# Folding the dt rows of an SSD layer to 128 partitions and moving two groups of transposes back in PE's queue

## The chip, the cores and the metric

The kernel runs on one core of one Trainium2 chip. The metric is device time in microseconds (us), the median over runs. All data are float32; the large products are done in three float32r matmuls (below).

## What is computed

A decoder trunk of two layers on 256 tokens with 2048 channels. Each layer is an RMSNorm with shift and scale from a conditioning vector (adaLN), a token mixer, an output projection, an adaLN gate and the residual sum. Layer 0 is a Mamba-2 SSD layer of 64 heads, layer 1 an xLSTM mLSTM layer of 8 heads. The part of the reference that the change touches is the step size dt of layer 0 and the decay that comes from it, in chunks of 128 tokens:

```python
proj = h @ w_in
z, xbc, dt = jnp.split(proj, [SSD_D_INNER, SSD_D_INNER + SSD_CONV_DIM], axis=-1)
dt = jax.nn.softplus(dt.astype(F32) + dt_bias.astype(F32))        # 256 tokens x 64 heads
a = -jnp.exp(a_log.astype(F32)).reshape(SSD_GROUPS, SSD_HEADS_PER_GROUP) * dt
y = ssd_chunked_scan(xs * dt[..., None], a, bmat, cmat)
# in the scan, for each chunk:
acs = jnp.cumsum(ac, axis=1)
decay = jnp.exp(jnp.where(causal, acs[:, :, None] - acs[:, None, :], -jnp.inf))
w_end = jnp.exp(total[:, None] - acs)
```

In layer 1 the input gate and the forget gate, one value per token and head, go through a log-sigmoid, a running sum and a running maximum in the same manner.

## The kernel before

**Tiling.** Weights stream from DRAM in tiles of 128x2048 floats, each loaded as two halves (`raw`, 128x1024). A half is split into two float32r parts: ACT copies it to `hi`, DVE subtracts to get `lo` (`split`, L270). A product is three matmuls: hi x h-hi, hi x h-lo, lo x h-hi (L304 to L306 with channels on the partitions, "fm"; L315 to L317 with tokens on the partitions, "tm"). There are six buffers for `raw` and four each for `hi` and `lo`. A half of an fm tile is 24 matmuls of 256 columns, a half of a tm tile 12 of 512.

**Units.** A `Unit` is one output block. It accumulates in two PSUM banks (the dt and gate units in one) of the pool `pj` or of the pool `ms` (function `misc()`), which have four banks each; small work shares `ms`: transposes, statistics, broadcasts. While the activations `h` of a layer come in four parts (adaLN scales arrive late), units are "parked": after each tile their two `ms` banks are added to a tile in SBUF by DVE (`park`, L86).

**Order.** The program is one list `items` of weight tiles, adaLN tiles and h parts. The main loop walks it half by half, issues loads and splits ahead, and before each half's matmuls steps every background generator once (`run_bg`). `yield` and `lag(n)` in a generator thus say how many halves later its next piece is issued. A scheduler then sets the order on each engine, and every engine takes its queue in order. The generators of the SSD heads wait by name (`held["dt"].over` and so on).

**The dt unit.** `dt_done` (L547) runs when the dt unit's 48 matmuls into one `pj` bank are issued. Its generator adds the bias and runs `softplus` (L413) on a 128x256 tile `dtrow`, of which only partitions 0 to 63 carry heads. One step later it multiplies by -exp(alog), scans each chunk of 128 tokens into `acs`, stores `acs` to DRAM (`acd`, POOL's queue) from where rows come back broadcast over partitions (`acb`, `gen_rows`), and computes `cr`, the distance to the chunk's end. One step after that come five PE transposes (L570 to L572) into two `ms` banks, and DVE copies them to `dtT` and `acT`, the per-token columns that `gen_decay` (ACT, tiles `E`) and `gen_ssd` (tiles `X`) use as scale and bias.

**The gate unit.** `gates_done` (L847) does the same for layer 1's gates: softplus on `gaterow`, scans, and after `lag(6)` four transposes (L872, L873) into two `ms` banks, read by ACT (`eT`) and DVE (`ncT`).

**Layer 1's moved products.** 16 adaLN tiles of layer 1 (`late`) are not loaded before layer 1 but dealt out between its first tiles, by the line with `n = ...` in the last loop over `items`.

## Time and profile before

| | us |
|---|---|
| median of 3 runs (1779.36 to 1780.19) | 1780.16 |
| the profiled execution | 1770.52 |
| its span, first to last instruction | 1768.7 |
| PE busy in it | 1679.2 |
| mean granted clock of PE | 0.98 of full |

The profile is of one execution. The span is what its rows add up to; 1.8 us of the profiled time lie around it. PE is the matmul engine, PEld its weight loads, DVE the vector engine, ACT the scalar engine, POOL and SP mostly issue DMAs here. [...] A row of the view in order of time gives start, duration, engine, line, operation, names out<-in, and in brackets how long the engine had been idle and who ended that. Durations of neighbours overlap by their pipeline's tail, so what an operation costs in a queue is the distance of two starts.

### The profile page before, as it was taken

The numbers are of one execution on the slowest core, as the hardware profiler recorded it, in microseconds if no ns is written. First come the engines' busy times: TensorE is split into PE (matmuls) and PEld (weight loads), VectorE is DVE, ScalarE is ACT, GpSimd is POOL, SyncE is SP. The second block draws the span as 40 slices with busy tenths as digits, with TensorE's granted clock in tenths as the row PEclk, the third lists the DMA queues.
The fourth block names the chain that finished last, engine by engine and source line by source line (L and its number), as shares of the span: only waits on it lengthen the run. The fifth ranks groups of instructions, "written<-read, shape, count | busy, mean of one in ns | idle before, by whom it ended". The sixth has DMA issues, their size and how long they took to land.

```text
span 1768.7 us, 32784 instructions
## 1 busy us (share of the span) xinstructions
PE 1679.2 (95%) x13285; PEld 1623.4 (92%) x13285; DVE 1301.9 (74%) x1639; ACT 923.3 (52%) x1551; POOL 35.6 (2%) x55
## 2 busy tenths in 40 slices
PE   2998979999999999989998999999999999999997
PEld 2998969998999999989888989899999898989997
DVE  7889978998986888867977986766556565564554
ACT  3443558788874674444445554544344444454433
POOL 0000000000000000000000000000000000000000
PEclk6999989999999999999999999999999999999998
DMA  9989745686876667958974567777555555565551
GB/s 358 338 311 320 275 161 179 213 280 226 280 284 207 220 219 254 337 167 307 328 249 153 203 229 246 254 246 246 182 181 178 181 175 184 188 196 169 189 180 71
DMA packets 111048, 405.20 MB, mean 229 GB/s; under 512 B 12440, under 2 KB 12448, under 8 KB 110896
## 3 DMA queue, kind: packets, MB, share of 16 engines
q1 hardware_dynamic: 107568, 391.50, 64.6%
q0 software_dynamic: 3040, 10.56, 2.0%
q8 instruction: 104, 1.70, 0.4%
q10 hardware_dynamic: 288, 1.05, 0.1%
q14 instruction: 48, 0.39, 0.1%
HBM read 400.89 MB, written 2.17 MB: 228 GB/s over the span
## 4 chain that ended last, share of the span: by engine, by line
PE 73%; issue 9%; DVE 8%; DMA 7%; ACT 2%; POOL 0%; SPq 0%; POOLq 0%; DVEq 0%; ACTq 0%
PE pj L304 18%; PE pj L305 18%; PE pj L306 18%; DMA raw<-in_ada 4%; DVE aacc L82 3%; DVE lo L86 3%; PE ms L304 2%; PE ms L305 2%; PE ms L306 2%; PE pj L315 2%; PE pj L317 2%; PE pj L316 2%; DMA raw<-in_wml 1%; ACT hi L78 1%; PE ms L697 1%
## 5 line engine op out<-in xcount | busy, mean ns | idle before, releaser
L78 ACT ACTIVATE hi<-raw 128x1024 fp32r<-128x1024 f32 x548 | 580.0, 1061 | 647.5 <-PE pj L305 394.0
L86 DVE TENSOR_TENSOR lo<-raw,hi 128x1024 fp32r<-128x1024 f32 x548 | 667.5, 1221 | 328.9 <-ACT hi L78 326.0
L304 PE MATMUL pj<-hT,hi 128*128 128x256 f32 x2144 | 605.3, 283 | 9.0 <-ACT hT L78 6.4
L305 PE MATMUL pj<-hT,hi 128*128 128x256 f32 x2144 | 600.3, 280 | 0.6 <-DVE hT L82 0.6
L306 PE MATMUL pj<-hT,lo 128*128 128x256 f32 x2144 | 600.0, 280 | 0.1
L304 PEld LDWEIGHTS pj<-hT,hi 128*128 128x128 f32 x2144 | 405.1, 189 | 12.2 <-ACT hT L78 7.2
L305 PEld LDWEIGHTS pj<-hT,hi 128*128 128x128 f32 x2144 | 405.1, 189 | 1.2 <-DVE hT L82 0.8
L306 PEld LDWEIGHTS pj<-hT,lo 128*128 128x128 f32 x2144 | 404.8, 189 | 0.3 <-DVE lo L86 0.3
L304 PE MATMUL pj<-y,hi 128*128 128x256 f32 x1024 | 291.4, 285 | 0.0
L306 PE MATMUL pj<-y,lo 128*128 128x256 f32 x1024 | 289.8, 283 | 0.0
L305 PE MATMUL pj<-y,hi 128*128 128x256 f32 x1024 | 289.8, 283 | 0.0
L82 DVE SCALAR_TENSOR_TENSOR aacc<-raw,cond,aacc 128x1024 f32<-128x1024 f32 x180 | 230.4, 1280 | 54.1 <-DMA raw<-in_ada 52.7
L304 PE MATMUL ms<-hT,hi 128*128 128x256 f32 x704 | 199.8, 284 | 9.4 <-ACT hi L78 3.3
L305 PE MATMUL ms<-hT,hi 128*128 128x256 f32 x704 | 197.6, 281 | 0.0
L306 PE MATMUL ms<-hT,lo 128*128 128x256 f32 x704 | 197.2, 281 | 0.0
L304 PEld LDWEIGHTS pj<-y,hi 128*128 128x128 f32 x1024 | 196.4, 192 | 0.5 <-issue 0.5
L305 PEld LDWEIGHTS pj<-y,hi 128*128 128x128 f32 x1024 | 196.5, 192 | 0.2 <-issue 0.2
L306 PEld LDWEIGHTS pj<-y,lo 128*128 128x128 f32 x1024 | 196.4, 192 | 0.0
L304 PEld LDWEIGHTS ms<-hT,hi 128*128 128x128 f32 x704 | 133.7, 190 | 12.1 <-ACT hi L78 4.6
L305 PEld LDWEIGHTS ms<-hT,hi 128*128 128x128 f32 x704 | 133.7, 190 | 0.3
L306 PEld LDWEIGHTS ms<-hT,lo 128*128 128x128 f32 x704 | 133.4, 190 | 0.0
L315 PE MATMUL pj<-hi,hT 128*128 128x512 f32 x192 | 76.5, 399 | 0.0
(186 smaller groups left out, 1549.3 us busy)
## 6 DMA issues: line engine op xcount, KB each, us to landing
raw<-in_wml SPq DMA_DIRECT2D x256, 512.0 KB, 4.2
raw<-in_ada SPq DMA_DIRECT2D x192, 512.0 KB, 5.3
raw<-in_wss SPq DMA_DIRECT2D x160, 512.0 KB, 4.8
raw<-in_wso SPq DMA_DIRECT2D x64, 512.0 KB, 5.8
raw<-in_wmo SPq DMA_DIRECT2D x64, 512.0 KB, 3.7
acb<-acd POOLq DMA_DIRECT2D x16, 512.0 KB, 5.6
xT<-in_xt SPq DMA_DIRECT2D x4, 512.0 KB, 5.9
raw<-in_wdt SPq DMA_DIRECT2D x2, 512.0 KB, 5.7
```

Of the source, the lines that this page charges most:

```text
L78: nc.scalar.activation(out, in_, func, **kw)
L82: nc.vector.scalar_tensor_tensor(out, a, s, b, op0, op1)
L86: nc.vector.tensor_tensor(out, a, b, op)
L304: nc.tensor.matmul(o, hi[:, w0:w0 + P], ah, start=first, stop=False, skip_group_check=True)
L305: nc.tensor.matmul(o, hi[:, w0:w0 + P], al, start=False, stop=False, skip_group_check=True)
L306: nc.tensor.matmul(o, lo[:, w0:w0 + P], ah, start=False, stop=last, skip_group_check=True)
L315: nc.tensor.matmul(o, ah[:, s], wh, start=(fresh and kk == 0), stop=False)
L316: nc.tensor.matmul(o, al[:, s], wh, start=False, stop=False)
L317: nc.tensor.matmul(o, ah[:, s], wl, start=False, stop=(kk == u.nk - 1 and (closes or (u.park is not None and ends))))
L697: nc.tensor.matmul(o, X[:, 0, xh, :], E[:, h, 0:T], start=True, stop=False, skip_group_check=True)
```

## The change

It does three things.

1. **dt.** After the bias, tokens 128 to 255 of the 64 heads are copied by ACT to partitions 64 to 127. `softplus`, the product with exp(alog) (now with the sign in the same operation, and exp(alog) copied to the upper partitions too) and the scan then run on 128x128. The scan's result lies in `dtrow` instead of `acs`; the store to DRAM is two stores of 64x128. The five transposes are three. They are issued after `lag(4)` instead of one step.
2. **Gates.** `lag(6)` becomes `lag(8)`.
3. **Layer 1's moved products.** The divisor of the line `n = ...` is smaller by 2.

```diff
--- before.py
+++ after.py
@@ -411,8 +411,9 @@
         return hT[:, k, 0:T], hT[:, k, T:2 * T]
 
     def softplus(x, out):
+        n = out.free_size()
         w = sp.tile([P, 3, T], F32, tag="e6", name=nm("spw"))
-        e, z, z2 = w[:, 0, :], w[:, 1, :], w[:, 2, :]
+        e, z, z2 = w[:, 0, 0:n], w[:, 1, 0:n], w[:, 2, 0:n]
         stt(e, x, -1.0, x, ALU.mult, ALU.min)
         act(e, e, AF.Exp)
         vts(z, e, 2.0, None, ALU.add)
@@ -537,7 +538,6 @@
 
     dtT = cp.tile([P, 2, 64], F32, tag="dtT", name="dtT")
     acT = cp.tile([P, 3, 64], F32, tag="acT", name="acT")
-    acs = cp.tile([P, T], F32, tag="rowA", name="acs")
     acd = dr.tile([64, T], F32, tag="acd", name="acd")
     dsk = cp.tile([P, 32], F32, tag="dskh", name="dskh")
     vts(dsk, vec("dsk", 0, 32), 0.5, None, ALU.mult)
@@ -548,32 +548,30 @@
         def g():
             bk = banks[0][:, 0:T]
             rw = sp.tile([P, 4, T], F32, tag="a4", name="dtrow")
-            dt, tmp = rw[:, 0, :], rw[:, 1, :]
-            vts(tmp, bk, vec("dtb"), None, ALU.add)
-            softplus(tmp, dt)
-            yield
-            na = sp.tile([P, 1], F32, tag="na", name="na", bufs=1)
-            act(na, vec("alog"), AF.Exp)
-            vts(na, na, -1.0, None, ALU.mult)
-            vts(tmp, dt, na, None, ALU.mult)
+            pre, dt, tmp, cr = rw[:, 0, :], rw[:, 1, 0:P], rw[:, 2, 0:P], rw[:, 3, 0:P]
+            acs = rw[:, 3, P:T]
+            vts(pre, bk, vec("dtb"), None, ALU.add)
+            act(pre[64:128, 0:P], pre[0:64, P:T], AF.Copy)
+            na = sp.tile([P, 2], F32, tag="na", name="na", bufs=1)
+            act(na[:, 0:1], vec("alog"), AF.Exp)
+            act(na[64:128, 0:1], na[0:64, 0:1], AF.Copy)
+            yield
+            softplus(pre[:, 0:P], dt)
+            stt(tmp, dt, -1.0, na[:, 0:1].broadcast_to([P, P]), ALU.mult, ALU.mult)
+            nc.vector.tensor_tensor_scan(acs, ones, tmp, 0.0, ALU.mult, ALU.add)
             for c in range(2):
-                s = slice(c * P, (c + 1) * P)
-                nc.vector.tensor_tensor_scan(acs[:, s], ones, tmp[:, s], 0.0, ALU.mult, ALU.add)
-            nc.gpsimd.dma_start(acd, acs[0:64, :])
+                nc.gpsimd.dma_start(acd[:, c * P:(c + 1) * P], acs[64 * c:64 * c + 64, :])
             slots.update(a4=1, e6=2)
             spawn(gen_rows())
-            cr = tmp[:, 0:P]
-            vts(cr, acs[:, 0:P], -1.0, acs[:, P - 1:P], ALU.mult, ALU.add)
-            yield
+            vts(cr, acs, -1.0, acs[:, P - 1:P], ALU.mult, ALU.add)
+            yield from lag(4)
             p1, p2 = misc(), misc()
-            for c in range(2):
-                nc.tensor.transpose(p1[:, c * P:(c + 1) * P], dt[:, c * P:(c + 1) * P], ident)
-                nc.tensor.transpose(p2[:, c * P:(c + 1) * P], acs[:, c * P:(c + 1) * P], ident)
-            nc.tensor.transpose(p2[:, 2 * P:3 * P], cr, ident)
+            nc.tensor.transpose(p1[:, 0:P], dt, ident)
+            nc.tensor.transpose(p2[:, 0:P], acs, ident)
+            nc.tensor.transpose(p2[:, P:T], cr, ident)
             give("a4")
-            vts(dtT, p1[:, 0:T].rearrange("p (c h) -> p c h", c=2)[:, :, 0:64],
-                                    0.5, None, ALU.mult)
-            nc.vector.tensor_copy(acT, p2[:, 0:384].rearrange("p (c h) -> p c h", c=3)[:, :, 0:64])
+            vts(dtT, p1[:, 0:P].rearrange("p (c h) -> p c h", c=2), 0.5, None, ALU.mult)
+            nc.vector.tensor_copy(acT, p2[:, 0:192].rearrange("p (c h) -> p c h", c=3))
             spawn(gen_decay())
             yield
         held["dt"] = spawn(g())
@@ -866,7 +864,7 @@
             nc.vector.tensor_tensor_scan(G, ip, ip, 0.0, ALU.max, ALU.max)
             nc.gpsimd.dma_start(Gd, G[0:8, :])
             vtt(lf, bc, G, ALU.add)
-            yield from lag(6)
+            yield from lag(8)
             p1, p2 = misc(), misc()
             for c in range(2):
                 nc.tensor.transpose(p1[:, c * P:(c + 1) * P], lf[:, c * P:(c + 1) * P], ident)
@@ -1012,7 +1010,7 @@
             if q == 3 and j == GPOS:
                 add_unit(Unit("fm", 1, 8, 1, h_act, gates_done), [wgt])
             items.append(w)
-            n = -(-len(late) // max(1, len(new) - j + (2 - q) * len(new))) if q < 3 and (q, j) >= (0, 3) else 0
+            n = -(-len(late) // max(1, len(new) - j + (2 - q) * len(new) - 2)) if q < 3 and (q, j) >= (0, 3) else 0
             items.extend(late[:n])
             late = late[n:]
     assert not late
```

What the built program makes of it is shown at three places, in the order of each engine's queue. Names carry buffer numbers, which differ between the two programs.

PE around the dt transposes, before (`pj340` is the dt unit's bank, `ms367` the first bank of the next tile, `hi350` its first half):

```order
L304 MATMUL pj340_2256<-hT_74,hi330_2188 128x256
L305 MATMUL pj340_2256<-hT_74,hi330_2188 128x256
L306 MATMUL pj340_2256<-hT_74,lo331_2189 128x256
L570 MATMUL ms355_2408<-ident_75,dtrow_2317 128x128 x2
L571 MATMUL ms356_2409<-ident_75,acs_164 128x128 x2
L572 MATMUL ms356_2409<-ident_75,dtrow_2317 128x128
L304 MATMUL ms367_2493<-hT_74,hi350_2363 128x256
L305 MATMUL ms367_2493<-hT_74,hi350_2363 128x256
```

And changed; between the dt unit and the first row here stand 44 matmuls of the next tile (`ms364`, `ms365`, halves `hi349` and `hi352`):

```order
L306 MATMUL ms365_2483<-hT_74,lo353_2400 128x256
L304 MATMUL ms365_2483<-hT_74,hi352_2399 128x256
L305 MATMUL ms365_2483<-hT_74,hi352_2399 128x256
L306 MATMUL ms365_2483<-hT_74,lo353_2400 128x256
L569 MATMUL ms370_2524<-ident_75,dtrow_2316 128x128
L570 MATMUL ms371_2525<-ident_75,dtrow_2316 128x128
L304 MATMUL ms376_2570<-hT_74,hi358_2438 128x256
L305 MATMUL ms376_2570<-hT_74,hi358_2438 128x256
L306 MATMUL ms376_2570<-hT_74,lo359_2439 128x256
L571 MATMUL ms371_2525<-ident_75,dtrow_2316 128x128
L304 MATMUL ms376_2570<-hT_74,hi358_2438 128x256
```

The transposes have moved behind two halves, 48 matmuls, and the third stands three matmuls behind the other two.

DVE in the softplus of dt, before (`spw` is softplus's work tile, `bc` and `xs` are convolutions of other units):

```order
L419 RECIPROCAL spw347_2319<-spw347_2319 128x256
L82 SCALAR_TENSOR_TENSOR bc365_2485<-th375_2565,bc365_2485 128x512
L86 TENSOR_TENSOR spw347_2319<-spw347_2319 128x256
L82 SCALAR_TENSOR_TENSOR xs354_2403<-pj60_300,V_72,xs354_2403 128x254
L86 TENSOR_TENSOR spw347_2319<-spw347_2319 128x256
L82 SCALAR_TENSOR_TENSOR xs354_2403<-pj60_300,V_72,xs354_2403 128x253
L90 TENSOR_SCALAR spw347_2319<-spw347_2319 128x256
L82 SCALAR_TENSOR_TENSOR bc365_2485<-pj68_362,V_72,bc365_2485 128x254
L82 SCALAR_TENSOR_TENSOR spw347_2319<-spw347_2319 128x256
L82 SCALAR_TENSOR_TENSOR bc365_2485<-pj68_362,V_72,bc365_2485 128x253
L82 SCALAR_TENSOR_TENSOR spw347_2319<-spw347_2319 128x256
L82 SCALAR_TENSOR_TENSOR xs354_2403<-th383_2617,xs354_2403 128x512
```

And changed, from the same operation on:

```order
L420 RECIPROCAL spw351_2354<-spw351_2354 128x128
L86 TENSOR_TENSOR lo369_2513<-raw347_2346,hi368_2512 128x1024
L86 TENSOR_TENSOR spw351_2354<-spw351_2354 128x128
L86 TENSOR_TENSOR park87_498<-park87_498,ms364_2482 128x512
L86 TENSOR_TENSOR spw351_2354<-spw351_2354 128x128
L86 TENSOR_TENSOR park87_498<-park87_498,ms365_2483 128x512
L90 TENSOR_SCALAR spw351_2354<-spw351_2354 128x128
L86 TENSOR_TENSOR lo374_2560<-raw348_2348,hi373_2559 128x1024
L82 SCALAR_TENSOR_TENSOR spw351_2354<-spw351_2354 128x128
L82 SCALAR_TENSOR_TENSOR bc362_2474<-th375_2563,bc362_2474 128x512
L82 SCALAR_TENSOR_TENSOR spw351_2354<-spw351_2354 128x128
L82 SCALAR_TENSOR_TENSOR xs354_2403<-pj60_299,V_72,xs354_2403 128x253
```

Every softplus operation is 128 wide, and two `lo` subtractions and two `park` additions stand between them, where convolution steps stood. Before, the corresponding subtractions and additions followed the transposes.

PE around the gate transposes, before (`ms1489`, `ms1490` belong to the tile before, `ms1501` to the next one):

```order
L316 MATMUL ms1490_11084<-hi1476_11004,hT_74 128x512
L317 MATMUL ms1490_11084<-lo1477_11005,hT_74 128x512
L872 MATMUL ms1498_11130<-ident_75,gaterow_10854 128x128
L873 MATMUL ms1499_11131<-ident_75,ip_10855 128x128
L872 MATMUL ms1498_11130<-ident_75,gaterow_10854 128x128
L873 MATMUL ms1499_11131<-ident_75,ip_10855 128x128
L304 MATMUL ms1501_11141<-hT_74,hi1483_11041 128x256
```

And changed, where 48 matmuls of the next tile (`ms1499`, `ms1500`) come first, and the tile after it (`ms1509`) follows:

```order
L305 MATMUL ms1500_11132<-hT_74,hi1486_11072 128x256
L306 MATMUL ms1500_11132<-hT_74,lo1487_11073 128x256
L870 MATMUL ms1507_11199<-ident_75,gaterow_10852 128x128
L871 MATMUL ms1508_11200<-ident_75,ip_10853 128x128
L870 MATMUL ms1507_11199<-ident_75,gaterow_10852 128x128
L871 MATMUL ms1508_11200<-ident_75,ip_10853 128x128
L315 MATMUL ms1509_11211<-hi1493_11099,hT_74 128x512
L316 MATMUL ms1509_11211<-hi1493_11099,hT_74 128x512
```

ACT at the same place, before:

```order
L78 ACTIVATE hi1493_11101<-raw1471_10971 128x1024
L78 ACTIVATE hi1496_11126<-raw1472_10973 128x1024
L78 ACTIVATE th1500_11138<-qk1488_11078 128x512
L78 ACTIVATE v1495_11123<-park1246_9433 128x512 x2
L78 ACTIVATE eT_169<-ms1498_11130 128x16
L78 ACTIVATE EP1529_11309<-Gb1507_11179,ncT_170 128x256
L78 ACTIVATE EP1529_11309<-Gb1507_11179,ncT_170 128x128
```

And changed:

```order
L78 ACTIVATE hi1493_11099<-raw1471_10969 128x1024
L78 ACTIVATE hi1496_11124<-raw1472_10971 128x1024
L78 ACTIVATE hi1503_11161<-raw1481_11035 128x1024
L78 ACTIVATE th1498_11128<-qk1488_11076 128x512
L78 ACTIVATE v1495_11121<-park1246_9431 128x512 x2
L78 ACTIVATE hi1505_11195<-raw1482_11037 128x1024
L78 ACTIVATE eT_168<-ms1507_11199 128x16
L78 ACTIVATE qk1517_11238<-park1267_9548,V_72 128x256 x3
```

`hi1503` stands ahead of the `v` copies and `hi1505` ahead of `eT`, and no `EP` operation, which waits for a DMA, stands right behind `eT`. Of the four `ms` banks, `ms1509` takes the one of `ms1507`, which `eT` reads.

On the load queue (SP) the two programs have the same order.

## Rows read from the trace of the kernel before

**Rows 1.** The page, part 1: busy us (share of the span) xinstructions.
```profile
PE 1679.2 (95%) x13285; PEld 1623.4 (92%) x13285; DVE 1301.9 (74%) x1639; ACT 923.3 (52%) x1551; POOL 35.6 (2%) x55
```

**Rows 2.** Waits, PE: engine line <- releaser: us in total, times, longest us.
```profile
PE ms L570 <- DVE dtrow L82: 12.9, 1, 12.9
...
PE ms L872 <- DVE gaterow L86: 5.3, 1, 5.3
```

**Rows 3.** Order of time, PE, 220 to 242: start us, us, instruction [idle before <-releaser].
```profile
220.86 0.36 PE L304 MATMUL pj<-hT,hi 128*128 128x256 f32 x1
...
226.43 0.27 PE L306 MATMUL pj<-hT,lo 128*128 128x256 f32 x1
239.59 0.69 PE L570 MATMUL ms<-ident,dtrow 128*128 128x128 f32 x2 [12.89 <-DVE dtrow L82]
...
241.09 0.56 PE L304 MATMUL ms<-hT,hi 128*128 128x256 f32 x1
```

**Rows 4.** Order of time, DVE, 226 to 242.
```profile
226.74 0.48 DVE L90 TENSOR_SCALAR dtrow<-pj,V 128x256 f32<-128x256 f32 x1 [0.20 <-PE pj L306]
227.14 0.47 DVE L82 SCALAR_TENSOR_TENSOR bc<-pj,V,bc 128x254 f32<-128x254 f32 x1
227.53 0.42 DVE L82 SCALAR_TENSOR_TENSOR spw<-dtrow 128x256 f32<-128x256 f32 x1
227.87 1.22 DVE L86 TENSOR_TENSOR lo<-raw,hi 128x1024 fp32r<-128x1024 f32 x1
229.00 0.29 DVE L90 TENSOR_SCALAR spw<-spw 128x256 f32<-128x256 f32 x1
229.20 0.47 DVE L82 SCALAR_TENSOR_TENSOR bc<-pj,V,bc 128x253 f32<-128x253 f32 x1
229.59 1.74 DVE L419 RECIPROCAL spw<-spw 128x256 f32<-128x256 f32 x1
231.25 0.63 DVE L82 SCALAR_TENSOR_TENSOR bc<-th,bc 128x512 f32<-128x512 f32 x1
...
239.12 0.42 DVE L82 SCALAR_TENSOR_TENSOR dtrow<-dtrow,spw 128x256 f32<-128x256 f32 x1
...
239.96 0.74 DVE L561 TENSOR_TENSOR_SCAN acs<-ones,dtrow 128x128 f32<-128x128 f32 x2
```

**Rows 5.** Order of time, PE, 956 to 971.
```profile
956.95 0.40 PE L317 MATMUL ms<-lo,hT 128*128 128x512 f32 x1
962.68 0.44 PE L872 MATMUL ms<-ident,gaterow 128*128 128x128 f32 x1 [5.33 <-DVE gaterow L86]
...
963.41 0.56 PE L304 MATMUL ms<-hT,hi 128*128 128x256 f32 x1
...
970.71 0.40 PE L315 MATMUL ms<-hi,hT 128*128 128x512 f32 x1
```

**Rows 6.** Order of time, DVE and ACT, 957 to 964.
```profile
962.46 0.67 DVE L86 TENSOR_TENSOR park<-park,ms 128x512 f32<-128x512 f32 x1
963.05 1.21 DVE L86 TENSOR_TENSOR lo<-raw,hi 128x1024 fp32r<-128x1024 f32 x1
...
957.20 1.06 ACT L78 ACTIVATE hi<-raw 128x1024 fp32r<-128x1024 f32 x1 [1.47 <-issue]
...
963.16 0.63 ACT L78 ACTIVATE v<-park 128x512 f32<-128x512 f32 x1 [0.30 <-DVE park L86]
963.70 0.17 ACT L78 ACTIVATE eT<-ms 128x16 f32<-128x16 f32 x1
```

**Rows 7.** Stretches: from:to us, length, busy us of five engines, PEclk, DMA share, GB/s.
```profile
245.00:480.00 235.00, 229.90 (x1966) 223.66 (x1964) 212.15 (x279) 195.34 (x441) 13.77 (x17) 1.00 0.70 236
417.00:424.00 7.00, 4.41 (x41) 3.89 (x40) 7.00 (x10) 3.70 (x9) 0.00 (x0) 1.00 0.87 270
962.60:966.90 4.30, 4.22 (x20) 4.25 (x21) 4.30 (x10) 0.96 (x3) 1.63 (x3) 0.50 0.41 122
```

**Rows 8.** Order of time, ACT, 247 to 252.
```profile
247.87 1.57 ACT L78 ACTIVATE E<-acb,acT 128x128 f32<-128x128 f32 x5 [1.73 <-DMA acb<-acd]
```

## The prediction

> **What bounds the kernel.** [...] The page's busy times come first: PE, the matmul engine, is busy for 95% of the span, DVE for 74% and ACT for 52% [rows 1]. A change pays here only where it removes time in which PE stands still, or in which it runs at its lower clock. Next, PE's waits, longest single wait first: two of them are for operands that this change touches, 12.9 us before the first dt transpose and 5.3 us before the first gate transpose [rows 2]. Both are single events. In PE's own order of time [rows 3, 5] one sees that PE had its next matmuls ready on both occasions: they follow the transposes without a further wait. So PE, which takes its queue in order, stood behind a transpose while work that did not need it was queued after it. [...]
>
> **The dt place, as it was.** The last dt matmul starts at 226.43, the first transpose at 239.59, the first matmul of the next tile at 241.09 [rows 3]. In between DVE is never idle: it works off the softplus, 256 columns an operation, with convolution steps of other blocks in between, from 226.74 to the last softplus step at 239.12 [rows 4].
>
> **The dt place, changed.** Two things happen. Half the columns: 128 partitions carry 128 tokens each. And by `lag(4)` 48 matmuls, two halves of a weight tile, now stand ahead of the first transpose. All four split halves lie ready (the matmuls after 241.09 ran on without a wait [rows 3]), so PE does these 48 in what was idle time. Their price: the dt unit is itself 48 such matmuls, from 220.86 to 226.43 plus one step, 5.6 us [rows 3].
>
> But the scheduler also drew other work forward into DVE's queue: two more `lo` subtractions and two `park` additions stand before the softplus ends. I price DVE's new queue, from the bias to the last softplus step, by start-to-start times of [rows 4]: the bias 0.40; eight convolution steps at 0.39, 3.1; three `lo` at 1.13, 3.4; two `park` additions at 0.59 [rows 6], 1.2; two silu products at 0.63, 1.3; two scalar steps at up to 0.20, 0.4; ten softplus steps of 128 columns; one reciprocal. No row shows 128 columns in those steps. 256 columns cost 0.34 [rows 4], which is the upper bound, and half of that, 0.17, the lower. The 512-column product and the 256-column step differ by 0.21 in duration [rows 4], so 128 columns less are worth about 0.12: I take 0.22, in all 2.2. The reciprocal costs 1.66 now, and I take half, 0.85. Sum 12.9; with 0.15 for the copy that folds the upper tokens (ACT's queue; between 0.17, a 128x16 operation [rows 6], and 0.31, a fifth of 1.57 [rows 8], mostly hidden behind two convolution steps) the last step begins at 239.8 where it began at 239.12. It is shorter by 0.12 until its result is there, so the first transpose comes 0.5 us later than before.
>
> The second transpose waits once more: DVE does the copy of dt and then the scan between the two, some 1.3 us with the first transpose's own time, plus 0.2 for the second. That makes 1.5 from the first transpose to matmul number 49. Before, it took 1.5 from 239.59 to 241.09 [rows 3] to matmul number 1. The third transpose, three matmuls later, costs 0.2 at the low clock. Gain at this place: 5.6 - 0.5 - 0.2 = **4.9 us**. If 128 columns cost as much as 256, the ten steps and the reciprocal are 2.0 longer: 2.9. If they cost half, 0.5 shorter: 5.4.
>
> [...]
>
> **The gate place.** The last matmul of the tile before starts at 956.95, the gate transposes at 962.68, and the next tile's 48 matmuls last from 963.41 to 970.71 [rows 5]: 7.3 us, because the clock was at 0.50 until 966.9 [rows 7]. With `lag(8)` these 48 come first. They begin at 957.3 at the full clock and end at 962.9. DVE had the transposes' operand ready for 962.68 [rows 5], and the addition that frees the second of their banks ends at about 963.1 [rows 6], so the transposes run almost at once, to 963.5. Then a new wait stands at the next tile: its first PSUM bank is that of a gate transpose, and is free when ACT has read `eT`. On ACT the second `v` copy still ends at 963.8 (its wait on DVE's second bank is unchanged), then one `hi` split now stands ahead of `eT`: about 1.0, and 0.17 for `eT` [rows 6]. PE goes on at 964.9 instead of 970.71. Gain **5.8 us**. It would be 7.2 without the new wait, and 3.7 if the next tile had to wait for both banks of the tile before, which DVE adds up only by about 967.
>
> **What costs nothing.** Layer 1's moved products: 16 late loads are dealt out over the tiles from the fourth on, as many per tile as a ceiling of (left)/(tiles left) gives. That is 16/21, 15/20 and so on before, 16/19, 15/18 and so on now; every one rounds up to 1. The order on the load queue is unchanged, so this edit does nothing. On POOL there is one more store of dt rows; what follows it is priced under the rivals. The two tiny additions at the start on ACT are bounded by 0.17 each [rows 6] and lie beside the wait for x. Behind both places PE is the bound (229.9 of 235 us with DMA at 0.70, [rows 7]), so what is gained stays gained; loads start when DVE or ACT frees their buffers, and move along.
>
> **Sum.** 4.9 + 5.8 = 10.7 us. The profiled execution took 1770.52, so it would take 1759.8; the median of the runs is 9.6 higher than the profiled one, which I carry over: 1780.16 - 10.7 = **1769.5**.
>
> **Rivals.**
> (a) The dt chain is as long per step as with 256 columns: gain 2.9 + 5.8, 1771.5. For it: nothing here shows 128 columns in these steps. Against it: 512 and 256 columns do differ. 12%.
> (b) The new short wait of 1.4 us at the gates, followed by another tile, brings the low clock back. In the rows of before it did not: the stretch with 2.6 us of no matmul kept 1.00 [rows 7]. If it did, the cost is that of the stretch after the old wait, half of 4.3 us: 2.1, so 1771.6. [...] 8%.
> (c) Layer 0's SSD work after dt is dealt out anew over all queues. PE now loses 5.1 us between 245 and 480 [rows 7]; a less lucky order could lose as much again: 1774.6. A luckier one could save half: 1767. 13% for the unlucky one.
> (d) The waits only change place, to the banks or to the second transpose, and under 3.6 us is left: about 1778. 7%.
> (e) Slower. ACT's queue holds, after dt, twelve E operations that wait for the dt rows to come back from DRAM, and the `hi` splits behind them. Those rows arrived at 247.87 [rows 8], 7.2 after the scan. Now the scan is later by about 0.7, and a second store goes first. PE has five halves, some 14 us, before it needs the split behind the E operations, which take about 4 us to get through: the rows may come by 251.5, some 2 us of slack. Each further microsecond costs one. To be slower by more than 0.2% (3.6 us, about what a measurement can tell from no change) they must be 16 us late; at 20 us the time is 1784. Nothing in the rows comes near it. 4%.
>
> **How the numbers follow.** My forecast has 56%. Faster by over 0.2% (below 1776.6) are the forecast, (a), (b) and most of (c): 88%. Within 0.2%: (d) and the rest of (c), 8%. Slower: (e), 4%. The range takes in both upper bounds with some luck in (c), 1764.5, and (a) together with (c), 1775: what lies outside has less than 2 in 10.
>
> **What would show it.** Right: PE's wait before the first dt transpose falls from 12.9 to about 8 us and a second one of about 1 us follows; 48 matmuls stand before them. The 5.3 us wait at the gates is gone, the clock there stays at 1.00, and a wait of about 1.4 us for `eT` appears. Wrong: a dt wait of 10 us or more (then the steps were not shortened), a low clock after the gates, or new waits on DVE between 245 and 500 that add up to several microseconds.

## The result and the profile after

The changed kernel took 1764.74 us (median of 4 runs, 1761.46 to 1765.99) where the kernel before took 1779.76 beside it: ratio 0.9912, 95% interval 0.9896 to 0.9927, by the ratio 15.7 us less (13.0 to 18.5). Measured a second time, against 23 runs of before, the ratio was 0.9935 (0.9920 to 0.9950), 11.6 us less. The forecast was 10.7 us less, 1769.5; the result is 4.8 below it, at the low end of the range of 1764.5 to 1775. The first interval excludes the forecast's ratio of 0.9940; the second holds it, close to its middle. So by how much the gain exceeds the forecast is open, from 1 to 5 us.

The page of the changed kernel, part 1, answers to [rows 1]: the busy times moved by 2.4 us or less. PE's rose by 1.6 while its span fell by 4.5 (1768.7 to 1764.2), so what went, in this pair of profiles, was idle time of PE.

```profile
PE 1680.8 (95%) x13283; PEld 1625.8 (92%) x13283; DVE 1299.7 (74%) x1637; ACT 924.9 (52%) x1553; POOL 36.0 (2%) x56
```

PE's waits of the changed kernel, for [rows 2]:

```profile
PE ms L569 <- DVE dtrow L82: 7.4, 1, 7.4
...
PE pj L304 <- DVE xs L82: 1.2, 1, 1.2
PE ms L315 <- ACT eT L78: 1.1, 1, 1.1
```

**The dt place.** PE in order of time; the 48 matmuls of the next tile end with the first row [rows 3]:

```profile
234.06 0.27 PE L306 MATMUL ms<-hT,lo 128*128 128x256 f32 x1
241.76 0.45 PE L569 MATMUL ms<-ident,dtrow 128*128 128x128 f32 x1 [7.42 <-DVE dtrow L82]
243.01 0.45 PE L570 MATMUL ms<-ident,dtrow 128*128 128x128 f32 x1 [0.81 <-DVE dtrow L561]
243.13 0.55 PE L304 MATMUL ms<-hT,hi 128*128 128x256 f32 x1
```

DVE in order of time, from the bias to the last softplus step [rows 4]:

```profile
228.78 0.48 DVE L90 TENSOR_SCALAR dtrow<-pj,V 128x256 f32<-128x256 f32 x1 [0.21 <-PE pj L306]
...
229.57 0.48 DVE L82 SCALAR_TENSOR_TENSOR xs<-pj,V,xs 128x254 f32<-128x254 f32 x1
230.09 0.29 DVE L82 SCALAR_TENSOR_TENSOR spw<-dtrow 128x128 f32<-128x128 f32 x1
...
231.96 0.94 DVE L420 RECIPROCAL spw<-spw 128x128 f32<-128x128 f32 x1
232.82 1.16 DVE L86 TENSOR_TENSOR lo<-raw,hi 128x1024 fp32r<-128x1024 f32 x1
...
238.75 0.28 DVE L82 SCALAR_TENSOR_TENSOR spw<-spw 128x128 f32<-128x128 f32 x1
238.95 0.47 DVE L82 SCALAR_TENSOR_TENSOR bc<-pj,V,bc 128x253 f32<-128x253 f32 x1
...
241.33 0.28 DVE L82 SCALAR_TENSOR_TENSOR dtrow<-dtrow,spw 128x128 f32<-128x128 f32 x1
```

From the bias to the last step it is 12.55 us; the forecast was 12.9 and 0.15 for the copy that folds the upper tokens. A step of 128 columns holds the queue for 0.20 (238.75 to 238.95; 0.22 assumed, 0.34 with 256), the reciprocal for 0.86. The copy, on ACT, ends where the first softplus step starts:

```profile
229.75 0.31 ACT L78 ACTIVATE dtrow<-dtrow 64x128 f32<-64x128 f32 x1
```

**The gate place.** PE, then ACT, in order of time [rows 5, 6]:

```profile
956.75 0.28 PE L304 MATMUL ms<-hT,hi 128*128 128x256 f32 x1
...
962.36 0.27 PE L870 MATMUL ms<-ident,gaterow 128*128 128x128 f32 x1
...
964.42 0.50 PE L315 MATMUL ms<-hi,hT 128*128 128x512 f32 x1 [1.13 <-ACT eT L78]
...
963.26 1.04 ACT L78 ACTIVATE hi<-raw 128x1024 fp32r<-128x1024 f32 x1
964.21 0.16 ACT L78 ACTIVATE eT<-ms 128x16 f32<-128x16 f32 x1
```

Stretches of the changed kernel (columns as in [rows 7]):

```profile
237.50:248.50 11.00, 5.94 (x28) 5.70 (x29) 7.66 (x23) 2.98 (x5) 2.37 (x4) 0.53 0.24 82
962.00:967.00 5.00, 3.76 (x20) 2.83 (x19) 5.00 (x9) 2.48 (x5) 1.66 (x4) 1.00 0.41 128
```

Of the two places only dt keeps a low clock: behind 7.42 us without a matmul it is at 0.53 in the 11 us from 237.5 (the last 4.3 us of that wait among them); at the gates it stays at 1.00 through the wait of 1.13.

**Where the time came from.** The 12384 product matmuls (L304 to L306, L315 to L317) run in the same order in both kernels, but for 75 that change places within one of the stretches below. So the distance from the start of one, counted from 0, to another measures the same work. Later runs gave four further profiles of the program before (five in all) and two of kernels that do what the changed one does (three in all; one of them, e4_u2, is a control described below). Worked out from their traces, mean and extremes in us:

```
matmul number                before, 5 profiles      changed, 3 profiles   difference
0-1200    up to dt           157.0 (155.4 - 158.5)   156.8 (156.4 - 157.1)   -0.2
1200-1536 dt place            57.7 (57.1 - 58.4)      53.0 (52.9 - 53.1)     -4.7
1536-2400                    117.6 (116.9 - 118.2)   117.9 (117.5 - 118.1)   +0.3
2400-3600 SSD behind dt      172.3 (170.8 - 175.3)   167.8 (167.0 - 168.1)   -4.5
3600-6600 to the gates       408.3 (406.4 - 410.6)   408.8 (407.1 - 410.8)   +0.4
6600-6750 gate place          31.3 (31.0 - 31.5)      25.3 (25.3 - 25.3)     -6.0
6750-12383 rest              777.4 (775.4 - 778.9)   776.9 (776.6 - 777.4)   -0.5
```

The dt place and the gate place gave about what the sum said, 4.9 and 5.8. A third stretch, 120 us behind dt, gave as much again, where the sum had nothing. Of this the first pair of profiles shows only part (170.8 to 168.1), because the profiled execution of before was the quickest of its five (1770.5; the others 1775.3, 1777.9, 1778.0 and 1786.7).

### The profile page after: what moved, and what is told of

Read it like the earlier page. It is cut to its first block, busy times and chain, and to the rows that moved or that the text cites. A ratio compares the mean times of both kernels' runs of the same rounds, so it can differ in the third digit from the quotient of the medians.

```text
span 1764.2 us, 32782 instructions
## 1 busy us (share of the span) xinstructions
PE 1680.8 (95%) x13283; PEld 1625.8 (92%) x13283; DVE 1299.7 (74%) x1637; ACT 924.9 (52%) x1553; POOL 36.0 (2%) x56
## 4 chain that ended last, share of the span: by engine, by line
PE 70%; issue 10%; DVE 9%; DMA 7%; ACT 2%; POOL 1%; SPq 0%; POOLq 0%; DVEq 0%; ACTq 0%
PE pj L304 17%; PE pj L305 17%; PE pj L306 17%; DMA raw<-in_ada 5%; DVE lo L86 3%; PE ms L304 3%; DVE aacc L82 3%; PE ms L305 3%; PE ms L306 3%; PE pj L315 2%; PE pj L317 2%; PE pj L316 2%; DMA raw<-in_wss 1%; ACT hi L78 1%; PE ms L957 1%
## 5 line engine op out<-in xcount | busy, mean ns | idle before, releaser
L304 PE MATMUL pj<-hT,hi 128*128 128x256 f32 x2144 | 606.1, 283 | 7.7 <-ACT hT L78 6.4
L306 PE MATMUL pj<-hT,lo 128*128 128x256 f32 x2144 | 600.2, 280 | 0.3 <-DVE lo L86 0.3
L304 PEld LDWEIGHTS pj<-hT,hi 128*128 128x128 f32 x2144 | 405.1, 189 | 11.0 <-ACT hT L78 7.2
L306 PEld LDWEIGHTS pj<-hT,lo 128*128 128x128 f32 x2144 | 404.9, 189 | 0.7 <-DVE lo L86 0.7
L304 PE MATMUL pj<-y,hi 128*128 128x256 f32 x1024 | 291.4, 285 | 0.0
L306 PE MATMUL pj<-y,lo 128*128 128x256 f32 x1024 | 289.7, 283 | 0.0
L304 PE MATMUL ms<-hT,hi 128*128 128x256 f32 x704 | 201.0, 286 | 7.6 <-ACT hi L78 4.5
L306 PE MATMUL ms<-hT,lo 128*128 128x256 f32 x704 | 198.5, 282 | 0.0
L304 PEld LDWEIGHTS pj<-y,hi 128*128 128x128 f32 x1024 | 196.4, 192 | 0.5 <-issue 0.5
L306 PEld LDWEIGHTS pj<-y,lo 128*128 128x128 f32 x1024 | 196.4, 192 | 0.0
L304 PEld LDWEIGHTS ms<-hT,hi 128*128 128x128 f32 x704 | 135.1, 192 | 10.0 <-ACT hi L78 5.3
L306 PEld LDWEIGHTS ms<-hT,lo 128*128 128x128 f32 x704 | 134.7, 191 | 0.0
L315 PE MATMUL pj<-hi,hT 128*128 128x512 f32 x192 | 76.6, 399 | 0.0
```

The lines of the kernel that those rows point to most:

```text
L304: nc.tensor.matmul(o, hi[:, w0:w0 + P], ah, start=first, stop=False, skip_group_check=True)
L306: nc.tensor.matmul(o, lo[:, w0:w0 + P], ah, start=False, stop=last, skip_group_check=True)
L315: nc.tensor.matmul(o, ah[:, s], wh, start=(fresh and kk == 0), stop=False)
```

## The experiments

### One part at a time

The divisor alone (e1_third):

```diff
-            n = -(-len(late) // max(1, len(new) - j + (2 - q) * len(new))) if ...
+            n = -(-len(late) // max(1, len(new) - j + (2 - q) * len(new) - 2)) if ...
```

> Only the divisor of the moved products is smaller by 2; the built program is the one of before, so this is a second look at the kernel before. Both theories expect a ratio of 1.000 within 0.001. Theory A (the profile of before is a fair one and the parts are worth 5 to 7 us each): the span of its profile is 1769 within 2 us. Theory B (an ordinary run of before is longer than its one profile, in the stretches that wait for adaLN loads: the first 200 us and the end of layer 0 to the start of layer 1, 780 to 900 us): the span is 1775 or more, and the extra time lies in these stretches, not at the dt or the gate transposes, whose waits stay 12.9 and 5.3 us.

1778.34, ratio 1.0005 (0.9991 to 1.0019). It builds the same program as before, and serves as a further profile of it: that of 1786.7, the longest of its 12 executions.

The gates alone (e1_gates):

```diff
-            yield from lag(6)
+            yield from lag(8)
             p1, p2 = misc(), misc()
             for c in range(2):
                 nc.tensor.transpose(p1[:, c * P:(c + 1) * P], lf[:, c * P:(c + 1) * P], ident)
```

> Only lag(6) is lag(8) for the gate transposes. Theory A: the next tile's 48 matmuls run before the transposes, the wait of 5.3 us and the low clock behind it go, a wait for eT of about 1.2 us comes: 5.8 us less, 1774 where before has 1779.8. Rival, that part of the 15 us comes from how the two parts act together or from a stretch that either part disturbs: clearly more than 7 us or under 4.

1772.52, ratio 0.9968 (0.9953 to 0.9982), 5.7 us less. Matmuls 6600 to 6750 take 25.3 us.

The dt edit alone (e1_dt: the fold and `lag(4)`, without the other two edits):

> Only the dt rows are folded and their transposes come after lag(4). Theory A: 5.5 us at the dt place (the wait of 12.9 becomes 7.4 and 0.8, with 48 matmuls done before) and 1.5 us in layer 0 behind it: 7 us less, 1773. Theory B: the rest of the 15 us is here, in layer 0 behind dt or at the layer boundary: 9 us or more less. Rival: the gain is given back before 500 us: under 4.

1767.84, ratio 0.9946 (0.9929 to 0.9962), 9.6 us less, twice the dt term of 4.9. Its dt place reads 52.9 in the trace, and matmuls 2400 to 3600 take 167.7. The interval of the time (6.8 to 12.6 us) excludes the dt term of 4.9. So a surplus comes with the dt edit, and in the trace it lies behind the dt place.

The changed kernel a second time (e1_again):

> The changed kernel as it is, once more. Theory A: about 1765, equal to the sum of the two parts alone within 1.5 us (12.8 less than before, or 15 if the parts are worth more than their rows). Theory B: the same time, but its profile differs from the first one of the changed kernel mostly in the first 200 us and between 780 and 900 us; at the dt place and at the gates both profiles agree within 0.5 us.

1765.98, the second ratio given at the top. The two parts alone, against the same runs of before, add up to 15.3 us where the whole gave 11.6; the intervals of the three reach just under 3 us to either side, too wide to say whether the parts add up.

### The fold and the lag apart

e2_fold is the fold with the transposes one step after the scan; e2_lag the old rows with the lag:

```diff
 # e2_fold, against the changed kernel (gates and divisor as before)
-            yield from lag(4)
+            yield
             p1, p2 = misc(), misc()
 # e2_lag, against the kernel before
-            yield
+            yield from lag(4)
             p1, p2 = misc(), misc()
```

> The fold alone: the dt rows on 128 partitions x 128 tokens, but the transposes one step after the scan as before, gates at lag(6), the old divisor. What is told apart is which of the two dt edits gave the gain at the dt place and which shortened PE's wait for the xs convolution near 420 us. Theory A (the queue position of the transposes does the work at the dt place): the fold only shortens the chain of ten softplus steps and a reciprocal by some 2 to 3 us, PE's wait before the first transpose falls from 12.9 to about 10.5, and since nothing stands in PE's queue ahead of it the time falls by 2 to 3 us there. If DVE's backlog is what PE waits for near 420, the fold, which takes a few us of work out of DVE's queue, also brings part of the 2.4 to 8 us behind dt: in all 1771 to 1775 where before is 1777.8. Rival B (half the columns is worth the gain, the lag little): 4 us or more at the dt place, 1768 to 1772. Rival C (128 columns cost as much as 256): 1777 to 1779.

> The lag alone: lag(4) ahead of the five old transposes, rows of 256 columns, gates at lag(6), the old divisor. Theory A: 48 matmuls, 5.6 us, go ahead of the first transpose; DVE's chain gets the extra lo subtractions and park additions, some 2 to 3 us, and keeps its 256 columns, so PE's wait before the first transpose is about 9 to 10 us and the gain at the place 2.5 to 4. Behind dt: if PE's wait near 420 us depends on how much DVE has to do, nothing is gained there, in all 1774 to 1775.5; if it depends on the order in which convolution steps and splits are dealt out, which the lag sets, it shrinks as in the full change, in all 1769 to 1772. Rival B (the lag does little without the fold): wait 11 us or more, 1777 or above.

PE's waits at the dt place, of e2_fold (first row) and of e2_lag:

```profile
PE ms L569 <- DVE dtrow L82: 10.7, 1, 10.7
```

```profile
PE ms L570 <- DVE dtrow L82: 9.2, 1, 9.2
...
PE ms L571 <- DVE acs L561: 0.7, 1, 0.7
```

The fold alone: 1775.92, ratio 0.9987 (0.9970 to 1.0004), 2.3 us less, with no change inside the interval; its dt place takes 55.5 where before has 57.7. The lag alone: 1771.94, ratio 0.9963 (0.9945 to 0.9981), 6.6 us less; its dt place takes 54.4, a gain of 3.3. The two together take the wait to 7.4 and 0.8. With the fold alone the stretch behind dt stays at 173.0, with the lag alone it is at 168.3: what shortens it is the lag.

What the lag changes there is DVE's queue. PE's wait in the profile of before that the forecast was made from, then DVE before, in order of time:

```profile
PE pj L304 <- DVE xs L82: 2.6, 1, 2.6
```

```profile
407.73 1.23 DVE L86 TENSOR_TENSOR y<-xs,y 128x1024 fp32r<-128x1024 f32 x1 [0.59 <-ACT y L78]
411.01 1.28 DVE L82 SCALAR_TENSOR_TENSOR aacc<-raw,cond,aacc 128x1024 f32<-128x1024 f32 x1 [2.06 <-DMA raw<-in_ada]
412.21 1.22 DVE L86 TENSOR_TENSOR lo<-raw,hi 128x1024 fp32r<-128x1024 f32 x1
413.35 0.99 DVE L82 SCALAR_TENSOR_TENSOR xs<-pj,V,xs 128x255 f32<-128x255 f32 x2
```

An adaLN accumulation stands at the head of DVE's queue, its load comes 2.06 us late, and the convolution steps of `xs`, whose end frees the `pj` bank for PE's next tile, stand behind it. PE then waits for them near 420 us: 2.6, 4.7, 2.9, 3.3 and 4.0 us in the five profiles of before, 1.2, 0.8 and 0.7 in the three of the changed kernel. (The run of the gates alone, whose queues up to there are those of before, had 1.8 and a stretch of 170.1.) After the waits of 4.7, 2.9 and 4.0 the clock fell as well, to 0.66, 0.86 and 0.88 in the 10 us from 427; after those of 2.6 and 3.3, and in the three of the changed kernel, it stayed at 1.00 there.

### The order behind dt by itself

e3_shift keeps the dt place of before and starts only the decay work later, which gives DVE the changed kernel's order near 410; e4_shift is the same kernel again:

```diff
             nc.vector.tensor_copy(acT, p2[:, 0:384].rearrange("p (c h) -> p c h", c=3)[:, :, 0:64])
+            yield from lag(3)
             spawn(gen_decay())
```

> The kernel before with nothing changed at the dt rows, the transposes or the gates; only behind the copies dtT and acT three more steps pass before the decay work is begun. So the dt place keeps its 57 to 58 us (matmul 1200 to 1536), while the SSD work behind it is dealt into the queues as with the lag. Near 410 us DVE then has six convolution steps of xs ahead of the adaLN accumulation that waits for a load, where the old order has two, so PE should no longer wait for them long. Theory A (the order alone gives the gain behind dt): PE's wait for xs near 420 us falls from 1.8 to 4.7 us to about 1.4 or less, the stretch from matmul 2400 to 3600 takes 167.5 to 169 us instead of 170 to 175, and the time is 3 to 5 us below before. Rival B (the gain behind dt comes from the time won at the dt place, as slack for loads or for DVE): the stretch stays at 170 to 175 and the time at that of before.

> The shift of the decay work in the kernel before (three more steps behind the copies, nothing else), the same kernel a second time, for a second estimate of its time. Theory A: 3 to 5 us below before, as the stretch from matmul 2400 to 3600 is again 167 to 169 us. Rival B: within 1.5 us of before, as the first time, although the stretch is short: then something else takes the time back in most executions.

DVE of e3_shift, the same place in order of time: five steps of the `xs` convolution and one other operation on `xs` now stand ahead of the accumulation, and it does not wait.

```profile
410.18 1.22 DVE L86 TENSOR_TENSOR lo<-raw,hi 128x1024 fp32r<-128x1024 f32 x1
411.31 0.48 DVE L82 SCALAR_TENSOR_TENSOR xs<-pj,V,xs 128x255 f32<-128x255 f32 x1
411.71 0.68 DVE L86 TENSOR_TENSOR xs<-xs,ms 128x512 f32<-128x512 f32 x1
412.30 1.64 DVE L82 SCALAR_TENSOR_TENSOR xs<-pj,V,xs 128x254 f32<-128x254 f32 x4
413.86 1.28 DVE L82 SCALAR_TENSOR_TENSOR aacc<-raw,cond,aacc 128x1024 f32<-128x1024 f32 x1
```

```profile
PE pj L304 <- DVE xs L82: 1.2, 1, 1.2
```

In both profiles PE waits 1.2 us there and the stretch takes 168.1 and 167.3, as theory A said. But the time did not follow: 1778.49, ratio 0.9992 (0.9978 to 1.0007), and 1778.99, ratio 1.0004 (0.9993 to 1.0016), which is the time of rival B. Some of it goes back at once (matmuls 1536 to 2400 take 118.6 and 118.1, 0.7 above the mean of before). Where the rest goes these profiles can't show: both are the quickest of their 12 executions (1770.89 and 1771.44), 7.6 us below the medians and no quicker than the quickest profile of before (1770.52). Whether the stretch is short in the usual execution too, and what then takes the gain back, stays open.

The reverse, in the changed kernel: e4_u3 delays the decay work so far that the accumulation falls ahead of the convolution again, e4_u2 delays it by one step less and keeps the changed kernel's order:

```diff
+            yield from lag(3)       # e4_u3; lag(2) in e4_u2
             spawn(gen_decay())
```

> The changed kernel, whole, with three more steps behind the copies dtT and acT before the decay work is begun. At the dt place nothing else changes. Near 410 us DVE's queue then stands as in the kernel before: an adaLN accumulation, which waits for its load, ahead of the xs convolution (one convolution step ahead of it, six in the changed kernel). Theory A (the order of DVE's queue behind dt is worth some 4 us of the gain): PE's wait for xs near 415 us is 2 us or more, the stretch from matmul 2400 to 3600 takes 170 to 174 us where the changed kernel has 168, and the time is 2 to 5 us above the changed kernel's 1765: 1767 to 1770. Rival B (the order is worth nothing in the timed runs, as the shift of the old kernel alone gave only 1.5 us): the same time as the changed kernel within 1.5 us, 1763.5 to 1766.5.

> The control to the run with three steps: two more steps behind the copies before the decay work is begun, which leaves DVE's order near 410 us as the changed kernel has it. Theory A: PE's wait for xs near 420 us stays at 0.8 to 1.9 us, the stretch from matmul 2400 to 3600 at 167 to 169 us, and the time at that of the changed kernel, 1763 to 1767. If the later start of the decay work by itself costs time, it is as long as with three steps, 1767 to 1770.

e4_u3 took 1767.68, ratio 0.9942 (0.9926 to 0.9958), e4_u2 1764.35, ratio 0.9928 (0.9908 to 0.9947). The difference of 2.5 us by the ratios has theory A's sign, but the intervals overlap. PE's wait near 417 in e4_u3 was 2.0 us, and the row names ACT, not DVE (the accumulation ahead of the convolution waited only 0.81 us for its load in this execution):

```profile
PE pj L304 <- ACT E L78: 2.0, 1, 2.0
```

Its stretch took 169.8, the control's 168.1.

### Further profiles of the kernel before

e5_b1, e5_b2 and e5_b3 are the kernel before, with no edit.

> The kernel before, unchanged, for a further profile. The one that the forecast was made from was an execution of 1770.5 where the timed ones lie at 1772 to 1786, and the one further profile of the same program (the divisor's run) took 1786.7. Theory A: in the usual execution the stretch from matmul 2400 to 3600 takes 171 to 175 us, with 2 to 5 us of PE's wait for xs near 420, and the dt place (matmul 1200 to 1536) 57 to 58.5. Rival B: the stretch is usually at 170 to 171, as in the first profile, and what makes the timed executions longer than the profiled one lies elsewhere (adaLN loads at the layer boundary, low clock past 840 us).

> The kernel before, unchanged, a third further profile, with the same expectations: theory A 171 to 175 us for the stretch from matmul 2400 to 3600, rival B 170 to 171.

> The kernel before, unchanged, a fourth further profile, with the same expectations: theory A 171 to 175 us for the stretch from matmul 2400 to 3600, rival B 170 to 171.

1775.28, 1777.99 and 1777.94; the stretch took 171.1, 171.1 and 173.1, between A and B, and the waits for `xs` are the 2.9, 3.3 and 4.0 above, the last of them:

```profile
PE pj L304 <- DVE xs L82: 4.0, 1, 4.0
```

So the stretch is 3 us (by the medians) to 4.5 us (by the means) longer before than after. What else sets the profiles apart lies at single events that come and go: matmuls 3600 to 6600 took from 406.4 to 410.6, and 7200 to 8000 took 114.1, 114.4, 116.9, 117.2 and 117.4.

### A longer lag

The changed kernel with `lag(5)`, `lag(6)`, `lag(7)` and `lag(8)` at the dt transposes (e3_lag5, e2_lag6 and e4_lag6, e3_lag7, e2_lag8):

```diff
-            yield from lag(4)
+            yield from lag(6)
             p1, p2 = misc(), misc()
```

> The full change with lag(6) for lag(4) at the dt transposes: two more halves (48 matmuls, 5.6 us) ahead of them. In the changed kernel PE still waited 7.4 and 0.8 us there and ran at half its clock for 10.2 us behind it. Theory A: the wait falls to 2 to 4 us, since the lag also puts more subtractions between the softplus steps; without a long wait the low clock stays away, which is worth up to 5 us more: 1756 to 1762 where the changed kernel is at 1766. Rival B (what is behind the transposes is the bound by now, the E operations that wait for acT and the split that stand behind them): the wait moves there, 1764 to 1767.

> The full change with lag(8) at the dt transposes: about 72 matmuls more ahead of them than in the changed kernel, 8.4 us. Theory A: no wait before the transposes and full clock, 1754 to 1760. Rival B: dt's columns dtT and acT now come 8 us later, ACT's E operations and the splits queued behind them are late, and PE waits for a split or for an X product in the next 20 us: no gain over lag(6), or a loss of 1 to 5 us against it.

> The full change with lag(7) at the dt transposes, between the two tried: about 72 matmuls more ahead of the first transpose than in the changed kernel. With lag(6) PE still waited 2.8 and 0.9 us and ran at half its clock for some 6 us behind it; with lag(8) these were gone but a wait of 1.6 us for dtT and one of 3.1 us for park came in their place, and the work behind was dealt in the unlucky order. Theory A: the waits before the transposes are under 1 us, the clock stays at 1.00, and the work behind keeps the order of lag(4): 1755 to 1759. Rival B: the work behind falls into the order of lag(8), 1760 to 1765.

> The full change with lag(5) at the dt transposes; 48 matmuls more than in the changed kernel stand ahead of the first transpose, as with lag(6), but the third transpose stands 6 matmuls closer. Theory A (the number of matmuls ahead of the first transpose sets the gain there): the same wait of 2.8 us as with lag(6) and 1758 to 1762. Rival B (the order behind dt, which turns on the step at which the decay work begins, decides): the dt place as with lag(6) but the stretch from matmul 2400 to 3600 back at 170 us or more, 1762 to 1766.

> The full change with lag(6) at the dt transposes a second time, as the version that may beat both kernels: 17 to 20 us below before again, and 2 to 5 us below the changed kernel; if the first time was luck, 14 to 16 below before, as the changed kernel.

`lag(6)` took 1759.62, ratio 0.9893 (0.9870 to 0.9917), and again 1762.51, ratio 0.9911 (0.9895 to 0.9927). `lag(5)`: 1764.40, 0.9914 (0.9901 to 0.9926). `lag(7)`: 1764.58, 0.9917 (0.9902 to 0.9932). `lag(8)`: 1763.49, 0.9904 (0.9880 to 0.9928). PE's waits from 225 to 275, with `lag(6)`, `lag(7)` and `lag(8)`:

```profile
PE ms L569 <- DVE dtrow L82: 2.8, 1, 2.8
PE ms L570 <- DVE dtrow L561: 0.9, 1, 0.9
```

```profile
PE ms L569 <- DVE dtrow L82: 2.8, 1, 2.8
PE ms L570 <- DVE dtrow L561: 1.8, 1, 1.8
PE ms L304 <- DVE park L86: 1.5, 1, 1.5
```

```profile
PE ms L304 <- DVE park L86: 3.1, 1, 3.1
PE ms L304 <- DVE dtT L90: 1.6, 1, 1.6
```

What I expected of `lag(5)` and `lag(7)` rested on a miscount: in their traces as many matmuls stand ahead of the first transpose as with `lag(4)` and `lag(6)`, so `lag(5)` has the old wait of 7.4 and the changed kernel's time, and `lag(7)` the 2.8 of `lag(6)`. `lag(6)` is the best of these: its two profiles take 166.6 us from matmul 1200 to 2400 where the changed kernel takes 170.8, and beside e4_u2 on the same chip it was 3 us quicker (0.9911 to 0.9928). In time its intervals overlap those of the changed kernel, and its second run, 15.8 us less than before, fell where its expectation had put a lucky first one (14 to 16). So a gain of 2 to 4 us over the changed kernel is likely, not proved. `lag(7)` meets theory B of its own run: it falls into the order with the accumulation ahead (stretch behind dt 172.7, wait for `xs` 2.9). With `lag(8)` the transposes' wait is gone and the clock stays at 1.00 until 262, but PE's bank comes late from `dtT` and `park` in its place.

## Why the prediction was right and wrong

**The dt term: its sum was right, two of its parts were not.** Forecast 4.9, measured 4.7 by the mean of the profiles (3.9 to 5.6 by their extremes). DVE's queue did better than forecast. The chain took 12.55 us and not 13.05, so the first transpose came 13.3 us behind the last dt matmul (228.46 to 241.76) where before it was 13.2 [rows 3]: 0.1 later, 0.5 forecast. From the first transpose to matmul number 49 it took 1.37, 1.5 forecast. Waits of 7.4 and 0.8 stand for the 8 and 1 that were named. The copy on ACT delayed the first softplus step by 0.13 (229.57 to 230.09, where a convolution step counts 0.39), 0.15 forecast.

The low clock behind the transposes did worse. The forecast left it as it was, but for 0.2 of the third transpose. The 48 matmuls behind the transposes took 6.6 to 8.0 us in the five profiles of before, 7.2 in the mean; the 48 behind the second transpose took 8.1, 8.3 and 8.2 in the three of the changed kernel. The clock in the 8 us from there, before and changed:

```profile
241.09:249.09 8.00, 8.00 (x62) 8.00 (x62) 2.86 (x4) 2.28 (x6) 1.76 (x3) 0.86 0.55 168
```

```profile
243.13:251.13 8.00, 8.00 (x50) 8.00 (x51) 3.61 (x7) 2.65 (x6) 2.37 (x4) 0.68 0.40 141
```

So the parts are 5.6 - 0.1 + 0.1 - 1.0 = 4.6. That 0.5 too much for the queue and 0.8 too little for the clock nearly cancel is luck. Why the clock came back later is not shown; in two of the five profiles of before the 48 took 8.0, nearly as long.

Rival (a) is out: a step counts 0.20, near the 0.22 that was chosen between 0.17 and 0.34. By its duration in the rows, 0.28 us for 128 columns and 0.42 for 256, a step would count more; but in the queue the next operation starts after 0.20 and 0.34, so the duration is not what an operation costs there. The time of the place can't tell the two apart: an estimate with 0.28 in place of 0.22 for each of the ten steps, 4.9 - 10 x 0.06 = 4.3, lies within its spread as 4.7 does.

**The gate term, right.** Forecast 5.8, measured 6.0 in the profiles and 5.7 in the time of that edit alone. The new wait for `eT` was 1.13 where about 1.4 was forecast, and PE went on 7.67 us after the tile's first matmul (956.75 to 964.42), 7.6 forecast. Rival (b) is out: the clock stayed at 1.00. The divisor does nothing, as forecast (e1_third).

**The step that failed: layer 0's SSD work behind dt, which was priced at nothing**, with 13% for an unlucky new order and its luckier side named only as "could save half: 1767". Nearly all of the surplus that the profiles show is there: 4.5 us by their means, 3 by their medians. Two things hid it. The rows of before showed the wait for `xs` (2.6 us, inside the stretch 417 to 424 of [rows 7]), but I did not follow it back to the accumulation on DVE and its late load, which would have shown that its size depends on what the lag deals ahead of it. And that wait differs from execution to execution: the one that I read had its shortest value of five, and I carried the 9.6 us by which the runs were longer over to the changed kernel unchanged. Such a gap is chance: the changed kernel's profiled execution lay 1.3 us above its median the first time (1765.99, 1764.74) and 5.6 below it the second (1760.34, 1765.98). The ends of the range were added up wrongly too: (a) with the whole of (c) is 1776.6, not 1775, and both upper bounds with half of (c) are 1765.0, where 1764.5 was written.

**What stays open.** In the lag's runs the surplus shows in the time as well (6.6 for the lag alone, of which 3.3 at its place; 9.6 for the dt edit, of which 4.7), but the same order in the old kernel left the time as it was, though the stretch was short in both its profiles, which are its quickest executions. Over all profiles, the ten with the changed kernel's order of DVE's queue near 410 us have a wait there of 0.6 to 1.9 us and a stretch of 167.0 to 168.7; the seven with the order of before have 1.8 to 4.7 and 170.1 to 175.3. So it is shown that the new dealing shortens the stretch, and the shift shows that the start of the decay work alone does it; DVE's order is argued from the rows to be the reason. That the stretch is the cause of the 1 to 5 us beyond the forecast is not shown. A gain at that wait which other chance events of the old kernel take back would look the same.

**The rivals on the other side.** Nothing of (d) and (e) appeared: ACT's E operations began at 250.29 where they began at 247.87 [rows 8], and no wait of PE for a split followed.

## What to carry to other kernels

When an edit moves a step of a generator, every queue behind it is dealt anew; price that by listing the waits that PE has there now, and following each back through the engine's queue to the transfer that starts it. A forecast made against one profiled execution should not carry the gap to the median over as a constant: the gap is made of chance waits, and the edit may move those too. The price of moved and narrowed work by start-to-start distances of neighbouring rows held to half a microsecond over a chain of 13; what a wait leaves behind in PE's clock needs a term of its own, here 1.0 us.

## What the runs showed of the hardware

A softplus step's duration in the trace overlaps its neighbour by 0.08 us: at 128 columns 0.28 last but 0.20 count, at 256 columns 0.42 and 0.34. A reciprocal of 128 columns counts 0.86, of 256 columns 1.66: half. And a wait of PE of nearly the same length can bring the lower clock or not: after 2.8 and 0.9 us of idle PE with `lag(6)` the next stretch ran at 0.67, after 2.7 and 1.0 in its second profile at 0.79; in the kernel before, the wait of 2.9 us near 420 was followed by 0.86 and a longer one, of 3.3, by 1.00. Stretches 244 to 252 of the two `lag(6)` profiles, first and second, then 427 to 437 of e5_b1 and e5_b2:

```profile
244.00:252.00 8.00, 7.76 (x47) 7.79 (x48) 5.71 (x13) 2.77 (x5) 2.37 (x4) 0.67 0.39 110
```

```profile
244.00:252.00 8.00, 7.53 (x51) 7.56 (x52) 6.38 (x13) 3.00 (x5) 2.37 (x4) 0.79 0.30 105
```

```profile
427.00:437.00 10.00, 10.00 (x77) 10.00 (x77) 10.00 (x15) 8.27 (x23) 0.53 (x1) 0.86 0.62 202
```

```profile
427.00:437.00 10.00, 9.42 (x83) 9.25 (x82) 10.00 (x14) 8.92 (x29) 1.54 (x2) 1.00 0.69 213
```
